# A hybrid decoder layer: the in-projection's first group in a hand-written order, meta tokens transposed together, gates in two passes

## Chip, cores and metric

The kernel runs on one core of one Trainium2 chip. The metric is device time in microseconds (us), the median of several runs. The engines are TensorE (PE, with its weight loads shown apart as PEld), VectorE (DVE), ScalarE (ACT), GpSimd (POOL) and SyncE (SP), which issues most DMAs.

## What is computed

One layer of a hybrid decoder trunk over 16 meta tokens and 256 real tokens of width 2048, in float32. The input is normalised by RMS and multiplied by a gain, then projected by `w_in` into all the inputs of an mLSTM, a stick-breaking attention and a pooling mixer. Their outputs are projected back, and a SwiGLU block follows. The part that matters here:

```python
xn = rmsnorm(h, g_pre)
u = jnp.einsum('bld,de->ble', xn, w_in) * vmask
ml_q, ml_k, ml_v, ml_o, ml_i, ml_f, sb_q, sb_k, sb_v, pool_u = split_cols(u, IN_SIZES)
log_i = jnp.where(vmask, ml_i + ig_b, -jnp.inf)
log_f = jnp.where(vmask, jax.nn.log_sigmoid(ml_f + fg_b), 0.0)
...
return h + token_mixing(h) + channel_mixing(...)   # meta tokens dropped at the end
```

`ml_i` and `ml_f` are the gates, six columns each.

## The kernel before

The contraction over 2048 is cut into 16 k tiles of 128. The activations lie transposed in SBUF, k on the partitions and 272 tokens (16 meta, 256 real) on the free axis. Each float32 operand is split into a high part in the multiplier's format and the rest (`xhi`, `xlo` for the tokens, `hi`, `lo` for the weights), and `mm3` makes a product from three matmuls: hi with hi, hi with lo, lo with hi. `split` makes the weight parts, the high one with a cast on ScalarE, the low one with a subtraction on VectorE. Only four such pairs of buffers exist, and three raw weight buffers.

The in-projection is a list of eleven groups of three or four blocks of 128 output columns, each block with an accumulator of its own in PSUM (`acc0` to `acc3`). The first group holds the blocks sbq0, sbq1 and sbq2 and, in `acc3`, the twelve gate columns. This group also has the work of getting started: a warm-up (eight products of ones with ones, L188, and the gain's transpose, L189), the transposes of x and of the meta tokens (`x_trans`, L209 to L218, three transposes to a k tile), the squares for the RMS (`x_squares`, twelve activations of 512 columns, L207), and `x_norm`, which turns the sums into 1/RMS per token and spreads it over the partitions with matmuls (L232) into `rb`. The gain is multiplied in when the transposed tile leaves PSUM; 1/RMS is multiplied in when a block's accumulator is read (`evac`, for sbq at L491).

The blocks go through chunks of k tiles (0-2, 2-4, 4-8, 8-12, 12-16). After each pair of k tiles the gates get three matmuls for each tile, with 38 weight columns: input gates at columns 0 to 5, forget gates at 32 to 37, and high and low weights in two separate tiles `gw[:, 0]` and `gw[:, 1]`, filled by small copies on ScalarE (L590) and subtractions on VectorE (L591). For the last chunk each block is finished before the next is begun, with `x_norm` behind the first block. `gates` (L281 on) then makes the mLSTM's gate sequences while the second group is running; it reads the gates' accumulator at L287 and, last, at L294. The second group has four blocks, so it needs all four accumulators.

The order on each engine is chosen by the compiler, which goes by its own forecast of times and by the order in the text; DMAs of x, of the meta tokens, of the gain and of the weight chunks are all issued by SP in the order of the text.

Of the kernel before, what the change touches and what calls it, by code (L numbers as in the profile page):

```python
# [37 lines left out]
def tile_hybrid_layer(  # L38
# [33 lines left out]
    def nm(s):  # L72
        uid[0] += 1
        return f"{s}_{uid[0]}"
# [9 lines left out]
    def load(view, nk, w):  # L84
        raw = rawp.tile([P, 2 * MB], F32, tag="raw", name=nm("raw"), bufs=RAWB)
        r = raw[:, : nk * w].rearrange("p (k c) -> p k c", c=w)
        sp.dma_start(out=r, in_=view)
        return r
# [22 lines left out]
    act.preload_act_table_set("natural_log_exp_and_others")  # L111
# [16 lines left out]
    x_v = x.rearrange("o (i p) d -> p (o i) d", p=P)  # L128
    row0 = wk.tile([P, 928], F32, tag="slot1", name="row0", bufs=1)[:16, :P]
# [13 lines left out]
    def load0(a, b):  # L143
        chunks[a] = load(win_view(a, b - a, OG, 396), b - a, 396)
# [16 lines left out]
    pool.dma_start(out=pw, in_=pool_w[0].rearrange("g c d -> c g d"))  # L161

# [16 lines left out]
    gw = big.tile([P, 2, KT, 64], F32R, tag="mixlo", name="gw")  # L179
    pool.memset(gw.bitcast(F32), 0.0)  # L180


    cols = cst.tile([P, 44], F32, name="cols")
    gmc = cst.tile([P, 16], F32, name="gmc")
    pc = mx()
    for _ in range(8):

        pe.matmul(pc[:, :P], lhsT=ones, rhs=ones, start=True, stop=True)  # L188
    pe.transpose(pc[:, :16], row0, ident[:16, :16])  # L189
    vec.tensor_copy(out=gmc, in_=pc[:, :16])  # L190
# [8 lines left out]
    ssx = mp.tile([P, 3, 4], F32, name="ssx")  # L199
    vec.memset(ssx, 0.0)  # L200

    def x_squares():
        for c in range(4):
            cs = slice(c * 512, (c + 1) * 512)
            for i, (src, n) in enumerate(((xin[:, 0, cs], P), (xin[:, 1, cs], P), (mt[:, cs], NMETA))):
                jk = wk.tile([P, 512], BF16, tag="jk", name=nm("jk"), bufs=1)
                act.activation(jk[:n], src, AF.Square, accum_out=ssx[:n, i, c : c + 1])  # L207

    def x_trans(k):  # L209
        pt = mx()  # L210
        ks = slice(k * P, (k + 1) * P)
        pe.transpose(pt[:, 0:NMETA], mt[:, ks], ident[:NMETA, :NMETA])
        pe.transpose(pt[:, NMETA : NMETA + P], xin[:, 0, ks], ident)
        pe.transpose(pt[:, NMETA + P : T], xin[:, 1, ks], ident)
        g = gmc[:, k : k + 1]
        act.activation(xhi[:, k, :], pt[:, :T], AF.Identity, scale=g)
        vec.scalar_tensor_tensor(out=xlo[:, k, :], in0=pt[:, :T], scalar=g, in1=xhi[:, k, :].bitcast(F32),
                                 op0=ALU.mult, op1=ALU.subtract)  # L218

# [61 lines left out]
    def gates(pg):  # L281
# [5 lines left out]
        vec.tensor_tensor(out=f[F], in0=pg[F, :T], in1=rb[F], op=ALU.mult)  # L287
# [6 lines left out]
        vec.tensor_tensor(out=ig[:NH], in0=pg[:NH, :T], in1=rb[:NH], op=ALU.mult)  # L294
# [268 lines left out]
    for gi, blocks in enumerate(groups):  # L563
        nb = len(blocks)
        w = P * nb
        accs = [acc(b) for b in range(nb)]
        pg = acc(3) if gi == 0 else None
        if gi == 0:
            spans = [(0, 2), (2, 4), (4, 8), (8, 12), (12, 16)]
        else:  # L570
            spans = [(4 * c, 4 * c + 4) for c in range(4)]
        for ka, kb in spans:
            if gi == 0:
                for k in range(0 if ka == 0 else kb, min(KT, 2 * kb if kb < 4 else kb + 4)):
                    x_trans(k)
                if ka == 8:
                    x_squares()
                    other_cols()
                r = chunks[ka] if ka in chunks else load(win_view(ka, kb - ka, OG, 396), kb - ka, 396)
            else:  # L580
                r = load_group(ka, kb, blocks)
            subs = []
            for k0 in range(ka, kb, 2):
                rs = r[:, k0 - ka : k0 - ka + 2]
                if gi == 0:
                    gsrc = rs[:, :, 0:12].rearrange("p k (a b) -> p k a b", a=2)
                    dst = [gw[:, j, k0 : k0 + 2, :].rearrange("p k (a b) -> p k a b", a=2)[:, :, :, 0:6]
                           for j in range(2)]
                    for a in range(2):
                        act.copy(out=dst[0][:, :, a], in_=gsrc[:, :, a])  # L590
                        vec.tensor_tensor(out=dst[1][:, :, a], in0=gsrc[:, :, a], in1=dst[0][:, :, a].bitcast(F32),  # L591
                                          op=ALU.subtract)
                    rs = rs[:, :, 12:]
                subs.append((k0, split(rs, 2, w)))
            last = kb == KT
            passes = [subs] if last else [[s] for s in subs]
            for ss in passes:
                for b, (kind, i) in enumerate(blocks):
# [9 lines left out]
                    if last:  # L608
                        if gi == 0 and b == 0:
                            x_norm()  # L610
# [325 lines left out]
```

## Time and profile before

| | us |
|---|---|
| median of 3 runs | 1122.26 (1122.12 to 1122.67) |
| the profiled execution | 1122.67 |
| its span | 1120.5 |
| TensorE busy | 1108.0 (99%) |
| VectorE busy | 700.3 (62%) |
| ScalarE busy | 501.4 (45%) |
| GpSimd busy | 22.8 (2%) |

The span runs from the first to the last instruction of the profiled execution; its time contains some 2.2 us more. Busy times of matmuls overlap, because a matmul is still draining when the next one starts: their pace is read from the spacing of their starts, not from their length. The clock column of the profile starts at full speed where it has no record yet, so in the first microseconds the spacing tells the clock better.

### The profile page before, as it was taken

To read this page: it belongs to the slowest core of one execution; us is meant where nothing else is said; L and a number is where in the kernel's file an instruction comes from. 1 tells how busy PE (TensorE), PEld (TensorE's weight loads), DVE (VectorE), ACT (ScalarE), POOL (GpSimd) and SP (SyncE) were. 2 spreads that over 40 slices of the span, in tenths; PEclk is the share of its full clock that TensorE was granted. 3 is DMA by queue.
4 is the path that set the end of the run, shared out by engine and by line. 5 is a ranking of instruction groups with operands and counts; after the bars stand their busy time and mean duration, and the time that the engine had idled before them with its cause. 6 is when DMAs were issued, how large, how long until landed. Compare 5 with 4: busy or idle time off the path is not lost.

```text
span 1120.5 us, 14565 instructions
## 1 busy us (share of the span) xinstructions
PE 1108.0 (99%) x5863; PEld 956.2 (85%) x5863; DVE 700.3 (62%) x932; ACT 501.4 (45%) x660; POOL 22.8 (2%) x66
## 2 busy tenths in 40 slices
PE   9999999999999999999999999999999999999997
PEld 7999999999988888888888888888888788888885
DVE  4776754768955766576585675774765844454444
ACT  6544444534434664444444444444344534343432
POOL 4000000000000000000000000000000000000000
PEclk9999999999999999999999999999999999999999
DMA  7554643544485655655656655656655555556652
GB/s 244 182 174 145 213 153 114 178 125 131 153 337 188 224 181 178 204 188 189 198 199 194 198 183 193 192 184 206 206 181 195 183 193 189 192 193 199 200 192 75
DMA packets 100548, 208.57 MB, mean 186 GB/s; under 512 B 3963, under 2 KB 31403, under 8 KB 99953
## 3 DMA queue, kind: packets, MB, share of 16 engines
q1 hardware_dynamic: 99168, 201.58, 55.0%
q0 software_dynamic: 896, 2.92, 0.9%
q10 hardware_dynamic: 416, 3.15, 0.7%
q8 instruction: 46, 0.75, 0.3%
q14 instruction: 22, 0.17, 0.0%
HBM read 205.52 MB, written 2.11 MB: 185 GB/s over the span
## 4 chain that ended last, share of the span: by engine, by line
PE 97%; DVE 2%; DMA 0%; ACT 0%; issue 0%; SPq 0%; DVEq 0%; POOLq 0%; ACTq 0%
PE mx L738 8%; PE mx L740 8%; PE mx L739 8%; PE acc L102 7%; PE acc L100 7%; PE acc L101 7%; PE acc L740 6%; PE acc L739 6%; PE acc L738 6%; PE mx L629 5%; PE mx L630 5%; PE mx L628 5%; PE acc L629 5%; PE acc L630 5%; PE acc L628 5%; DVE lo L96 1%
## 5 line engine op out<-in xcount | busy, mean ns | idle before, releaser
L96 DVE TENSOR_TENSOR lo<-raw,hi 128x1024 fp32r<-128x1024 f32 (+1 forms) x384 | 459.1, 1200 | 356.2 <-ACT hi L95 353.2
L95 ACT CAST hi<-raw 128x1024 fp32r<-128x1024 f32 (+1 forms) x384 | 393.8, 1029 | 489.9 <-PE mx L740 124.3
L102 PE MATMUL acc<-xhi,lo 128*128 128x272 f32 (+4 forms) x640 | 192.2, 301 | 0.0
L100 PE MATMUL acc<-xhi,hi 128*128 128x272 f32 (+4 forms) x640 | 187.2, 292 | 0.4 <-DVE im L294 0.4
L101 PE MATMUL acc<-xlo,hi 128*128 128x272 f32 (+4 forms) x640 | 186.7, 292 | 0.0
L738 PE MATMUL mx<-hi,x2hi 128*128 128x512 f32 x384 | 149.6, 390 | 0.0
L740 PE MATMUL mx<-hi,x2lo 128*128 128x512 f32 x384 | 149.6, 390 | 0.0
L739 PE MATMUL mx<-lo,x2hi 128*128 128x512 f32 x384 | 149.4, 389 | 0.0
L738 PE MATMUL acc<-hi,x2hi 128*128 128x512 f32 x320 | 124.5, 389 | 0.0
L739 PE MATMUL acc<-lo,x2hi 128*128 128x512 f32 x320 | 124.5, 389 | 0.0
L740 PE MATMUL acc<-hi,x2lo 128*128 128x512 f32 x320 | 124.5, 389 | 0.0
L100 PEld LDWEIGHTS acc<-xhi,hi 128*128 128x128 f32 x640 | 121.5, 190 | 2.2 <-issue 1.4
L102 PEld LDWEIGHTS acc<-xhi,lo 128*128 128x128 f32 x640 | 121.5, 190 | 1.6 <-issue 1.0
L101 PEld LDWEIGHTS acc<-xlo,hi 128*128 128x128 f32 x640 | 121.4, 190 | 0.3
L738 PEld LDWEIGHTS mx<-hi,x2hi 128*128 128x128 f32 x384 | 72.1, 188 | 15.0 <-ACT x2hi L832 0.3
L740 PEld LDWEIGHTS mx<-hi,x2lo 128*128 128x128 f32 x384 | 72.1, 188 | 14.9
L739 PEld LDWEIGHTS mx<-lo,x2hi 128*128 128x128 f32 x384 | 72.1, 188 | 14.8
L771 DVE STREAM_TRANSPOSE turn<-hg 32x256 f32<-32x256 f32 x176 | 76.7, 436 | 2.8
L739 PEld LDWEIGHTS acc<-lo,x2hi 128*128 128x128 f32 x320 | 60.1, 188 | 12.6
L738 PEld LDWEIGHTS acc<-hi,x2hi 128*128 128x128 f32 x320 | 60.1, 188 | 12.4
L740 PEld LDWEIGHTS acc<-hi,x2lo 128*128 128x128 f32 x320 | 60.1, 188 | 12.4
L629 PE MATMUL acc<-lo,hid 128*128 128x512 f32 x176 | 68.7, 390 | 1.4 <-DVE lo L96 1.4
(225 smaller groups left out, 1252.4 us busy)
## 6 DMA issues: line engine op xcount, KB each, us to landing
raw<-in_w_gate_up_dram SPq DMA_DIRECT2D x88, 1024.0 KB, 5.1
raw<-in_w_down_dram SPq DMA_DIRECT2D x44, 1024.0 KB, 5.2
raw<-in_w_in_dram SPq DMA_DIRECT2D x36, 512.0 KB, 4.8
raw<-in_w_out_dram SPq DMA_DIRECT2D x16, 1024.0 KB, 5.2
raw<-in_w_in_dram SPq DMA_DIRECT2D x12, 1024.0 KB, 5.2
raw<-in_w_in_dram SPq DMA_DIRECT2D x8, 768.0 KB, 4.5
raw<-in_w_in_dram SPq DMA_DIRECT2D x3, 792.0 KB, 6.9
h<-in_x_dram ACTq DMA_DIRECT2D x1, 2048.0 KB, 11.7
```

Source lines behind the costliest of these rows:

```text
L95: act.copy(out=h, in_=r)
L96: vec.tensor_tensor(out=l, in0=r, in1=h.bitcast(F32), op=ALU.subtract)
L100: pe.matmul(o, lhsT=wh, rhs=xh, start=start, stop=False, **kw)
L101: pe.matmul(o, lhsT=wh, rhs=xl, start=False, stop=False, **kw)
L102: pe.matmul(o, lhsT=wl, rhs=xh, start=False, stop=stop, **kw)
L628: pe.matmul(o, lhsT=lh, rhs=h[:, 0, js], start=k == 0, stop=False)
L629: pe.matmul(o, lhsT=lh, rhs=l[:, 0, js], start=False, stop=False)
L630: pe.matmul(o, lhsT=ll, rhs=h[:, 0, js], start=False, stop=k == nk - 1)
L738: pe.matmul(o, lhsT=x2hi[:, k, ts], rhs=h[:, kk, :], start=k == 0, stop=False)
L739: pe.matmul(o, lhsT=x2hi[:, k, ts], rhs=l[:, kk, :], start=False, stop=False)
L740: pe.matmul(o, lhsT=x2lo[:, k, ts], rhs=h[:, kk, :], start=False, stop=k == KT - 1)
L771: vec.transpose(out=dst[32 * j : 32 * j + 32, :, :, a, :], in_=src[32 * a : 32 * a + 32, :, :, j, :])
```

## The change

The first group gets a function of its own, `first_group`, in a region (`manual_schedule`) in which TensorE, ScalarE and VectorE execute in the order of the text. Meta tokens are loaded a second time in the layout (8 k tiles x 16 tokens) x 128 columns and transposed in two transposes instead of sixteen. The gate weights' high and low parts lie side by side in one tile of 102 columns, so that each k tile takes two matmuls instead of three (the product of the two low parts is computed too), and `gates` adds the two halves. The squares are taken in two calls of three activations of 1024 columns, behind the pairs 12 and 14. The warm-up has eleven products, five ahead of the gain's transpose and six behind it. The gain row and the first weight chunk are issued by ScalarE, the meta rows behind the x slices.

```diff
-    sp.dma_start(out=row0, in_=g_mix_pre.rearrange("o (a b) -> (o a) b", b=P))
     load_x(0, 2)
-    sp.dma_start(out=mt, in_=meta)
-    load0(0, 2)
+    act.dma_start(out=row0, in_=g_mix_pre.rearrange("o (a b) -> (o a) b", b=P))
+    load0(0, 2, act)
     load_x(2, 4)
     load0(2, 4)
     load_x(4, 8)
     load0(4, 8)
+    for h in range(2):
+        sp.dma_start(out=mt8[:, h, :], in_=meta[:, h * 1024 : (h + 1) * 1024].rearrange("t (k c) -> k t c", c=P))
     load_x(8, 12)
     load_x(12, 16)
+    sp.dma_start(out=mt, in_=meta)
...
+    gw = big.tile([P, KT, P], F32R, tag="mixlo", name="gw")
+    pool.memset(gw.bitcast(F32), 0.0)
+    act.preload_act_table_set("natural_log_exp_and_others")
...
+    def warm(pc, n):
+        for _ in range(n):
+            pe.matmul(pc[:, P : 2 * P], lhsT=ones, rhs=ones, start=True, stop=True)
+    def gain_column():
+        pc = mx()
+        warm(pc, 5)
+        pe.transpose(pc[:, :16], row0, ident[:16, :16])
+        vec.tensor_copy(out=gmc, in_=pc[:, :16])
+        warm(pc, 6)
...
+    def x_squares(c):
+        cs = slice(c * 1024, (c + 1) * 1024)
+        for i, (src, n) in enumerate(((xin[:, 0, cs], P), (xin[:, 1, cs], P), (mt[:, cs], NMETA))):
+            jk = wk.tile([P, 1024], BF16, tag="jk", name=nm("jk"), bufs=1)
+            act.activation(jk[:n], src, AF.Square, accum_out=ssx[:n, i, c : c + 1])
...
     def x_trans(k):
         pt = mx()
-        pe.transpose(pt[:, 0:NMETA], mt[:, ks], ident[:NMETA, :NMETA])
-        pe.transpose(pt[:, NMETA : NMETA + P], xin[:, 0, ks], ident)
-        pe.transpose(pt[:, NMETA + P : T], xin[:, 1, ks], ident)
+        pe.transpose(pt[:, 0:P], xin[:, 0, ks], ident)
+        pe.transpose(pt[:, P : 2 * P], xin[:, 1, ks], ident)
...
+    def meta_trans():
+        pt = mx()
+        for h in range(2):
+            pe.transpose(pt[:, h * P : (h + 1) * P], mt8[:, h, :], ident)
+        mg = itile(NT).rearrange("p (k t) -> p k t", t=NMETA)
+        vec.tensor_tensor(out=mg, in0=pt[:, : 2 * P].rearrange("p (k t) -> p k t", t=NMETA),
+                          in1=gmc.unsqueeze(2).broadcast_to([P, KT, NMETA]), op=ALU.mult)
+        vec.tensor_copy(out=xhi[:, :, 0:NMETA], in_=mg)
+        vec.tensor_tensor(out=xlo[:, :, 0:NMETA], in0=mg, in1=xhi[:, :, 0:NMETA].bitcast(F32), op=ALU.subtract)
...
-        vec.tensor_tensor(out=f[F], in0=pg[F, :T], in1=rb[F], op=ALU.mult)
+        act.copy(out=e[F], in_=pg[96:102, :T])
+        act.copy(out=ig[:NH], in_=pg[64:70, :T])
+        vec.tensor_tensor(out=f[F], in0=pg[F, :T], in1=e[F], op=ALU.add)
+        vec.tensor_tensor(out=f[F], in0=f[F], in1=rb[F], op=ALU.mult)
...
-        vec.tensor_tensor(out=ig[:NH], in0=pg[:NH, :T], in1=rb[:NH], op=ALU.mult)
+        vec.tensor_tensor(out=ig[:NH], in0=pg[:NH, :T], in1=ig[:NH], op=ALU.add)
+        vec.tensor_tensor(out=ig[:NH], in0=ig[:NH], in1=rb[:NH], op=ALU.mult)
...
+        def w_gates(ka, kb):
+            gsrc = chunks[ka][:, :, 0:12].rearrange("p k (a b) -> p k a b", a=2)
+            dst = gw[:, ka:kb, :].rearrange("p k (s a b) -> p k s a b", s=2, a=2)[:, :, :, :, 0:6]
+            vec.tensor_copy(out=dst[:, :, 0], in_=gsrc)
+            vec.tensor_tensor(out=dst[:, :, 1], in0=gsrc, in1=dst[:, :, 0].bitcast(F32), op=ALU.subtract)
+        def gate_pair(k0):
+            for k in (k0, k0 + 1):
+                pe.matmul(pg[:102, :T], lhsT=gw[:, k, 0:102], rhs=xhi[:, k, :], start=k == 0, stop=False)
+                pe.matmul(pg[:102, :T], lhsT=gw[:, k, 0:102], rhs=xlo[:, k, :], start=False, stop=k == KT - 1)
+        with tc.manual_schedule(engines={mybir.EngineType.PE, mybir.EngineType.Activation, mybir.EngineType.DVE}):
+            gain_column()
+            x_pair(0)
+            w_pair(0)
+            x_pair(2)
+            w_gates(0, 2)
+            w_pair(2)
+            pair(0)
+            x_pair(4)
+            w_gates(2, 4)
+            w_pair(4)
+            pair(2)
+            x_pair(6)
+            w_pair(6)
+            w_gates(4, 8)
+            pair(4)
+            meta_trans()
+            x_pair(8)
+            w_pair(8)
+            pair(6)
+            for k in (0, 2, 4, 6):
+                gate_pair(k)
+            x_pair(10)
+            w_pair(10)
+            w_gates(8, 12)
+            pair(8)
+            gate_pair(8)
+            x_pair(12)
+            w_pair(12)
+            x_squares(0)
+            pair(10)
+            gate_pair(10)
+            x_pair(14)
+            w_pair(14)
+            w_gates(12, 16)
+            x_squares(1)
+            other_cols()
+            for b in range(3):
+                products(accs, blocks, b, [(k, subs[k]) for k in (12, 14)])
+                if b == 0:
+                    x_norm()
+                    gate_pair(12)
+                    gate_pair(14)
+                evac(*blocks[b], accs[b])
+        quick.append([0, gates(pg), None])
```

`x_pair(k)` transposes the tiles k and k+1, `w_pair(k)` splits their weights, `pair(k)` runs their products for the three blocks, 18 matmuls.

## Rows read from the trace of the kernel before

**Rows 1.** Windows: stretch, busy us of each engine (instructions), TensorE clock, DMA share, GB/s.

```profile
42.40:48.00 5.60, 5.22 (x44) 5.04 (x43) 4.03 (x8) 1.71 (x4) 0.00 (x0) 1.00 0.49 148
60.00:1000.00 940.00, 938.38 (x4968) 811.99 (x4967) 610.56 (x802) 423.59 (x535) 6.94 (x11) 1.00 0.57 187
```

**Rows 2.** Timeline of TensorE, 0 to 14 us: start, length, engine, line, operation.

```profile
1.13 3.78 PE L188 MATMUL mx<-ones 128*128 128x128 f32 x16 [1.13 <-DVE ssx L200]
...
6.62 0.28 PE L212 MATMUL mx<-ident,mt 16*128 16x16 f32 x1 [1.50 <-DMA mt<-in_meta_tokens_dram]
...
9.67 0.56 PE L100 MATMUL acc<-xhi,hi 128*128 128x256 f32 x1
...
13.55 0.41 PE L102 MATMUL acc<-xhi,lo 128*128 128x256 f32 x1
```

**Rows 3.** Timeline of TensorE, 14 to 25 us.

```profile
14.46 0.23 PE L212 MATMUL mx<-ident,mt 16*128 16x16 f32 x1
14.62 0.33 PE L213 MATMUL mx<-ident,xin 128*128 128x128 f32 x1
...
14.99 0.23 PE L212 MATMUL mx<-ident,mt 16*128 16x16 f32 x1
...
22.08 0.28 PE L100 MATMUL acc<-xhi,hi 128*128 128x256 f32 x1
...
23.85 0.29 PE L100 MATMUL acc<-xhi,gw 128*38 128x272 f32 x1
...
24.60 0.28 PE L100 MATMUL acc<-xhi,hi 128*128 128x256 f32 x1
```

**Rows 4.** Timeline of TensorE, 37 to 48 us: end of group one, second group.

```profile
37.10 0.93 PE L232 MATMUL mx<-im,ones 128*128 128x128 f32 x6
...
42.39 0.28 PE L100 MATMUL acc<-xhi,hi 128*128 128x260 f32 x1
...
46.56 0.28 PE L102 MATMUL acc<-xhi,lo 128*128 128x256 f32 x1
47.23 0.36 PE L100 MATMUL acc<-xhi,hi 128*128 128x256 f32 x1 [0.38 <-DVE im L294]
```

**Rows 5.** Timeline of ScalarE, 11 to 32 us.

```profile
11.12 0.64 ACT L207 ACTIVATE jk<-xin 128x512 bf16<-128x512 f32 x1
...
11.88 0.63 ACT L207 ACTIVATE jk<-mt 16x512 bf16<-16x512 f32 x1
...
20.33 2.08 ACT L216 ACTIVATE xhi<-mx,gmc 128x272 fp32r<-128x272 f32 x4 [0.19 <-PE mx L214]
...
27.21 0.19 ACT L207 ACTIVATION_READ_ACCUMULATOR jk<-mt 16x1 f32 x1
...
30.17 0.83 ACT L95 CAST hi<-raw 128x768 fp32r<-128x768 f32 x1
30.89 0.30 ACT L590 CAST gw<-raw 128x12 fp32r<-128x12 f32 x2
```

**Rows 6.** Groups by line and form, 0 to 90 us: busy us, mean ns.

```profile
L95 ACT CAST hi<-raw 128x1024 fp32r<-128x1024 f32 x18 | 18.6, 1046 | 22.8 <-PE acc L101 22.8
```

**Rows 7.** DMA issues, 0 to 60 us: KB each, median us to landing.

```profile
xin<-in_x_dram SPq DMA_DIRECT2D x2, 256.0 KB, 4.9
```

**Rows 8.** Waits of SP's queue, 0 to 70 us: us in total, times, longest.

```profile
SPq L87 <- DVE gw L591: 9.8, 2, 9.1
```

**Rows 9.** Timeline of VectorE, 30 to 35 us.

```profile
31.03 0.96 DVE L96 TENSOR_TENSOR lo<-raw,hi 128x768 fp32r<-128x768 f32 x1
...
33.97 0.61 DVE L231 TENSOR_SCALAR im<-ident,r 128x128 f32<-128x128 f32 x3
```

**Rows 10.** Timeline of GpSimd, 26 to 30 us.

```profile
27.88 0.89 POOL L116 TENSOR_TENSOR r<-s,neghalf 128x3 f32<-128x3 f32 x1 [13.64 <-DVE s L115]
```

**Rows 11.** Windows at the end of the kernel, columns as in rows 1.

```profile
1112.00:1114.00 2.00, 0.61 (x3) 0.19 (x1) 0.91 (x3) 0.69 (x2) 0.26 (x1) 1.00 0.74 272
...
1116.50:1117.00 0.50, 0.00 (x0) 0.00 (x0) 0.50 (x2) 0.00 (x0) 0.00 (x0) 0.52 0.99 374
```

More of the change, by code (lines that the diff above doesn't have):

```diff
@@ L196, in other_cols @@
         vec.tensor_copy(out=cols, in_=pc[:, :44])
-    ssx = mp.tile([P, 3, 4], F32, name="ssx")
+    ssx = mp.tile([P, 3, 2], F32, name="ssx")
     vec.memset(ssx, 0.0)
[L202 to L207, printed above, removed]
+    def x_squares(c):
[3 more added lines that the diff above has]
+            act.activation(jk[:n], src, AF.Square, accum_out=ssx[:n, i, c : c + 1])
     def x_trans(k):
@@ L561, in load_group, with products, first_group, x_pair @@
         return r
-    for gi, blocks in enumerate(groups):
+    def products(accs, blocks, b, subs):
+        kind, i = blocks[b]
+        ts = slice(first(kind, i), T)
+        bs = slice(b * P, (b + 1) * P)
+        for k0, (h, l) in subs:
+            for kk in range(2):
+                k = k0 + kk
+                mm3(accs[b][:, : T - ts.start], h[:, kk, bs], l[:, kk, bs], xhi[:, k, ts], xlo[:, k, ts],
+                    k == 0, k == KT - 1)
+            tick()
+    def first_group(blocks):
+        accs, pg = [acc(b) for b in range(3)], acc(3)
+        subs = {}
+        def x_pair(k):
+            x_trans(k)
+            x_trans(k + 1)
+        def w_pair(k):
+            ka = k if k < 4 else k // 4 * 4
+            if k == ka and ka not in chunks:
+                chunks[ka] = load(win_view(ka, 4, OG, 396), 4, 396)
+            subs[k] = split(chunks[ka][:, k - ka : k - ka + 2, 12:], 2, 384)
+        def w_gates(ka, kb):
[3 more added lines that the diff above has]
+            vec.tensor_tensor(out=dst[:, :, 1], in0=gsrc, in1=dst[:, :, 0].bitcast(F32), op=ALU.subtract)
+        def pair(k):
+            for b in range(3):
+                products(accs, blocks, b, [(k, subs[k])])
+        def gate_pair(k0):
[39 more added lines that the diff above has]
+            other_cols()
+            for b in range(3):
+                products(accs, blocks, b, [(k, subs[k]) for k in (12, 14)])
[5 more added lines that the diff above has]
+        quick.append([0, gates(pg), None])
@@ L564, in tile_hybrid_layer @@
+    first_group(groups[0])
+    for blocks in groups[1:]:
         nb = len(blocks)
-        w = P * nb
         accs = [acc(b) for b in range(nb)]
[L567 to L597, printed above, removed]
-                for b, (kind, i) in enumerate(blocks):
-                    ts = slice(first(kind, i), T)
-                    n = T - ts.start
-                    for k0, (h, l) in ss:
-                        for kk in range(2):
-                            k = k0 + kk
-                            bs = slice(b * P, (b + 1) * P)
-                            mm3(accs[b][:, :n], h[:, kk, bs], l[:, kk, bs], xhi[:, k, ts], xlo[:, k, ts],
-                                k == 0, k == KT - 1)
-                        tick()
@@ L608, in tile_hybrid_layer @@
+        for ka in range(0, KT, 4):
+            r = load_group(ka, ka + 4, blocks)
+            subs = [(k0, split(r[:, k0 - ka : k0 - ka + 2], 2, P * nb)) for k0 in (ka, ka + 2)]
+            last = ka + 4 == KT
+            for ss in [subs] if last else [[s] for s in subs]:
+                for b, (kind, i) in enumerate(blocks):
+                    products(accs, blocks, b, ss)
                     if last:
-                        if gi == 0 and b == 0:
-                            x_norm()
```

28 lines of the change are left out of this document (7 added, 21 removed).

## The prediction

> **What bounds the kernel.** I read the windows first. In the long middle TensorE is busy 938.38 of 940.00 us [rows 1], so whatever the first group of the in-projection gains or loses stays in the total: nothing behind it has slack to swallow it. The change touches only that first group, so the question is when TensorE starts the second group. Before, that is at 42.39 us [rows 4]. Then I read TensorE's timeline from the start. It runs eight warm-up products (3.78 us, 0.47 each), pauses until 6.62 for the meta tokens, transposes four k tiles, and begins the products at 9.67 [rows 2]. From there to 42.39 it has no wait. A product of 256 columns comes every 0.23 us from 9.67 to 13.55 (17 steps) and every 0.118 us later (15 steps from 22.08 to 23.85) [rows 2, 3]: about what 256 columns take at 1.2 and at 2.4 GHz, so the clock rose at about 13.8 us. The one wait near the seam stands in the second group: 46.56 + 0.12 to 47.23, about 0.55 us, for the gates' last read of their accumulator [rows 4]; the window there shows 5.22 us busy of 5.60 [rows 1].
>
> ScalarE and VectorE had slack because the compiler slipped the row squares into gaps. The change takes that freedom away: three engines now run the first group in the order written. So I laid each engine's queue out by hand from row durations.
>
> **Work removed from TensorE.** Meta transposes: 16 go, two come. One takes 0.16 us (14.46 to 14.62) of a set of three that takes 0.53 [rows 3]. At that level 16 x 0.16 = 2.6 us go; each new one costs half of the remaining 0.37, so 0.4 comes, net -2.2. Gates: 48 products become 32, at 0.125 us (six from 23.85 to 24.60) [rows 3]: -2.0. Their weights grow from 38 to 102 columns; the nearest row on the other side is the main product, whose 128-column weights step at 0.118 us, so I charge nothing.
>
> **The start.** Five warm-ups (2.35 us from 1.13), a gain transpose (0.28, the level of the meta transposes in [rows 2]), six more (2.82): TensorE is free at about 6.6, where it was at 6.62 before [rows 2]. The first x slice no longer queues behind other loads; issued near 0.8 with a landing time of 4.9 [rows 7], it is there by 5.7, so the longer warm-up eats that head start. The gain row and the first weight chunk move to ScalarE's queue, idle then. The two new meta loads and the other x slices land as before or earlier, and the plain meta rows, now last, are first read near 31 us. The weight chunks of k 8 and 12, whose issue waited 9.8 us for the gate copies [rows 8], come earlier. The gate copies leave ScalarE: ten small operations on VectorE, 0.2 us each by the diagonal of 128 columns in [rows 9], in gaps that my layout leaves there. Clearing the gate tile and loading ScalarE's table move within the first 7 us, ahead of whatever reads them. Where loads share engines a slice may land 1 us later; that is a bound, +0 to +0.5.
>
> From 6.6: x_pair(0) ends its first tile at 7.0; with 0.2 for the drain, two gains on ScalarE at 0.52 (four in 2.08) end at 8.2, the cast of the weights 0.72 (30.17 to 30.89) at 8.9 [rows 5], its low part 0.96 [rows 9] at about 9.9. Two products pass before that, sixteen follow: 9.9 + 16 x 0.118 = 11.8, if the clock is high.
>
> **To the squares.** From 11.8 TensorE has the transposes of five pairs (4, 6, 8, 10, 12) at 4 x 0.185 = 3.7 us, four pairs of products at 18 x 0.118 = 8.5, the meta tokens 0.4, and 20 gate products 2.5: 15.1, so the tiles of k 12 and 13 are transposed at 26.9. None of these waits in my layout: ScalarE idles 1 to 3 us ahead of each pair. (If the meta tokens' strided write into all k rows is held against the reads of neighbouring columns, add up to 1.0 us; I take none, since the column ranges do not meet.)
>
> **The squares, where the gain goes.** In the written order x_squares(0) stands on ScalarE behind the cast of pair 12 and ahead of the gains of pair 14; x_squares(1) stands behind the cast of pair 14; and x_norm's three products stand on TensorE between the last block of sbq0 and everything else. A square with its read of the sum costs 0.76 us at 512 columns (11.12 to 11.88) [rows 5]. At 1024 no row shows it: bounded by 0.76 and twice that. The cast of 1024 takes 1.05 [rows 6] against 0.83 for 768 [rows 5], 0.22 for 256 columns, so I take 0.76 + 0.43 = 1.19, three for 3.6.
>
> ScalarE: the gains of 12 and 13 end 27.8; cast 28.5; squares 32.1; gains of 14 and 15 33.1; cast 33.8; squares 37.4. Then the sums: in the trace the last read ends at 27.21 + 0.19 = 27.40 and the root is done at 27.88 + 0.89 = 28.77 [rows 5, 10], so 1.37: 38.8. The first diagonal 0.2 (three in 0.61) [rows 9]: 39.0. TensorE's x_norm 0.93 [rows 4]: 39.9. Behind it wait 8 gate products (1.0) and 24 products (2.8): the second group starts at 43.7. TensorE itself would have been at the pair 14 products at 31.3 (26.9, then 2.1 of pair 10, 0.5 of gates, 0.7 of transposes, 0.2 of other_cols, 0.7 of pair 12); it waits 2.5 for the cast, 0.8 for the low part and 3.6 for x_norm, some 7 us, more than the change removes.
>
> **The sum.** 43.7 - 42.39 = +1.3. The 0.55 wait in the second group should go: the gates' sums are whole at 40.9, before two blocks of products, so two copies and one more add fit ahead of the 48.0 at which the fourth accumulator is wanted (43.7 + the 4.3 of [rows 4], 42.39 to 46.68). Bound: 0 to -0.55; I take all. In sum +0.75. The profiled execution took 1122.67 us (span 1120.5 and 2.2 around it), 0.4 over the median of 1122.26; the same difference on the median gives 1123.0. Own range of this case: squares of 1.0 to 1.45 move it by -1.1 to +1.6, so 1121.9 to 1124.6. A measurement of this kernel can tell about 0.2%, 2.2 us, from no change, so this case is mostly "same".
>
> **Rivals.**
> *The warm-up does not lift the clock (slower).* My sum needs TensorE at the high level by the first products. In the trace 3.78 us of warm-up and a pause did not lift it; 3.05 us of transposes and 4.1 of products without a break did [rows 2]. The new warm-up is 5.4 us with a transpose in it, running straight into transposes: longer than the one that failed, shorter than the stretch that worked. If it stays low until the products have run about 4 us, 18 products cost 0.11 more each: +2.0, so +2.8 and 1125.0. Against: no pause of 1.5 us stands in it now. Chance 0.27.
>
> *The squares do not hold TensorE (faster).* If ScalarE clears them before TensorE reaches x_norm, the last block goes on when the low part of pair 14 is there: transposes end 30.4, gains 31.6, cast 32.3, low part 33.3, six products 0.7, x_norm 0.9, 3.8 of the rest: 38.7, and with the wait gone -4.2, 1118.0. It decides where the squares end before 32.5. For it: before, they were done by 27.40 [rows 5], fitted between casts, and ScalarE is idle ahead of every pair. Against: the order on the engine is written out, and a half-size effect (one of the two calls out of the way) gives only about 1120. Chance 0.16.
>
> *The clock falls during the wait (slower).* TensorE would stand 3.6 us before x_norm. At the end of the kernel its last product ends at about 1112.6 and the granted clock falls only at about 1116.5 (0.52 over the half microsecond from there) [rows 11]: 3.9 us of idleness, just over what I lay out. If it falls, the 32 products behind x_norm run at 0.23 for 0.12, up to 3.5 us more, about +3 if it rises again before the end: 1126. The Trainium skill (TensorE: Matmul & The Clock Gate, "Why this matters for your kernels") speaks against this change here: it warns that long idle gaps between bursts of matmuls put the clock back to half. By that rule the time would be the 1126 just given; the tail row agrees with the rule in kind, and shows the clock still high for as long as this wait lasts. Chance 0.05.
>
> *The squares are cheaper and nothing else moves*: the lower end of the forecast's own range, 1121.9, within its 0.52.
>
> **Numbers.** Forecast 0.52, clock late 0.27, squares free 0.16, clock falls 0.05. Of the forecast nearly all lies within 0.2%, the clock and wait cases lie above it but for 0.01, the free squares below. Faster 0.17, same 0.52, slower 0.31. The range 1119.8 to 1125.4 leaves out about 0.1 below and 0.1 above.
>
> **What would show it.** Right: TensorE waits in front of the pair 14 products on the cast, then in front of x_norm on the diagonals, 6 to 8 us in all; ScalarE runs six 1024-wide squares between about 28 and 38 us without a gap; second group starts near 43.7; no wait on the gates at the fourth accumulator. The clock step is read from the spacing of the first products, 0.118 or 0.21. Wrong: a start of the second group before 41, or squares done before 31, would mean that the hold was mis-read; products at 0.21 beyond 10 us give the clock case.

## The result, and the profile after

The changed kernel takes 1129.65 us (median of 6 runs, 1127.27 to 1131.32); beside it the kernel before took 1122.55. The ratio is 1.006, with a 95% interval of 1.005 to 1.007: slower by 0.6%, where 1123.0 with a range to 1125.4 was forecast. The profiled execution took 1127.27 us, with a span of 1125.4; it is the quickest of the six. Two more executions, profiled later, took 1131.9 each and are read below.

All of the loss is made in the first group. Counted from the end of the kernel, the same matmul starts 5.2 us later than before at 51 us and still 5.0 us later at 1108 us. So the question is again when the second group starts. The waits of the first 60 us (engine and line, what it waited for: us in total, times, longest):

```profile
PE mx L251 <- DVE im L250: 5.2, 1, 5.2
...
PE acc L102 <- DVE lo L96: 3.0, 3, 1.9
PE acc L100 <- ACT hi L95: 2.9, 2, 2.1
```

The timeline of TensorE shows where these stand; it answers to [rows 2 to 4].

```profile
4.12 2.06 PE L193 MATMUL mx<-ones 128*128 128x128 f32 x12 [0.27 <-DVE gmc L199]
6.01 0.27 PE L222 MATMUL mx<-ident,xin 128*128 128x128 f32 x1
...
9.17 0.39 PE L102 MATMUL acc<-xhi,lo 128*128 128x256 f32 x1 [0.61 <-DVE lo L96]
...
16.46 0.38 PE L102 MATMUL acc<-xhi,lo 128*128 128x256 f32 x1 [1.92 <-DVE lo L96]
...
26.60 0.37 PE L624 MATMUL acc<-xhi,gw 128*102 128x272 f32 x1 [0.65 <-DVE gw L616]
...
34.06 0.38 PE L100 MATMUL acc<-xhi,hi 128*128 128x256 f32 x1 [2.14 <-ACT hi L95]
35.05 0.38 PE L102 MATMUL acc<-xhi,lo 128*128 128x256 f32 x1 [0.49 <-DVE lo L96]
40.96 1.73 PE L251 MATMUL mx<-im,ones 128*128 128x128 f32 x6 [5.17 <-DVE im L250]
...
48.06 0.29 PE L100 MATMUL acc<-xhi,hi 128*128 128x260 f32 x1
```

The second group starts at 48.06, where it was 42.39 before [rows 4] and 43.7 was forecast. The waits at 34, 35 and 41 us were forecast (2.5, 0.8 and 3.6); the ones at 16.46 and 26.60 were not. The cause of the first stands on VectorE (first fence), while GpSimd clears buffers (second fence):

```profile
9.82 0.25 DVE L615 CAST gw<-raw 128x24 fp32r<-128x24 f32 x1
...
12.89 2.44 DVE L615 CAST gw<-raw 128x24 fp32r<-128x24 f32 x1
15.36 0.18 DVE L616 TENSOR_TENSOR gw<-raw,gw 128x24 fp32r<-128x24 f32 x1
15.46 0.95 DVE L96 TENSOR_TENSOR lo<-raw,hi 128x768 fp32r<-128x768 f32 x1
```

```profile
11.20 0.84 POOL L273 MEMSET sbk<- 128x112 f32 x6
...
12.40 1.57 POOL L275 MEMSET mlq<- 128x256 f32 x6
...
14.80 0.95 POOL L277 MEMSET mlv<- 128x128 f32 x6
```

A copy of 24 columns takes 0.25 us before the clears and 2.44 us among them (it ends at 15.33, the last clears at 15.75); the low part of pair 4 queues behind it, and TensorE waits for that. At 26.60 TensorE waits for the gate weights of the tiles 8 to 11, whose copy stands on VectorE behind the low part of pair 10. Then ScalarE's squares, which answer to [rows 5]:

```profile
31.43 1.06 ACT L217 ACTIVATE jk<-mt 16x1024 bf16<-16x1024 f32 x1
...
33.92 1.05 ACT L217 ACTIVATE jk<-xin 128x1024 bf16<-128x1024 f32 x1
...
34.97 1.03 ACT L95 CAST hi<-raw 128x1024 fp32r<-128x1024 f32 x1
35.90 1.05 ACT L217 ACTIVATE jk<-xin 128x1024 bf16<-128x1024 f32 x1
...
36.95 1.03 ACT L95 CAST hi<-raw 128x1024 fp32r<-128x1024 f32 x1
37.89 1.05 ACT L217 ACTIVATE jk<-mt 16x1024 bf16<-16x1024 f32 x1
38.85 0.18 ACT L217 ACTIVATION_READ_ACCUMULATOR jk<-mt 16x1 f32 x1
```

Two casts of 1024 columns, work of the second group, stand between the last three squares. The hand-written order holds among the instructions of the region; the casts come from the text behind it, and the compiler has put them in. The windows (columns as in [rows 1]) show the clock:

```profile
34.00:36.00 2.00, 1.23 (x6) 0.83 (x6) 1.38 (x4) 2.00 (x5) 0.00 (x0) 0.95 0.00 0
36.00:38.00 2.00, 0.00 (x0) 0.00 (x0) 1.23 (x1) 2.00 (x4) 0.00 (x0) 0.50 0.67 170
...
44.00:46.00 2.00, 2.00 (x11) 2.00 (x10) 0.40 (x1) 0.76 (x2) 0.00 (x0) 0.50 0.04 10
46.00:48.00 2.00, 2.00 (x19) 2.00 (x18) 1.56 (x5) 0.57 (x1) 0.00 (x0) 0.99 0.01 4
```

It falls to 1.2 GHz near 35.8 us and comes back near 46.0, so everything behind `x_norm` up to there runs at half pace: 11 matmuls in the window from 44, 19 in the next.

### The profile page after: what moved, and what is told of

It reads as the page before. It is cut to its first block, busy times and chain, and to the rows that moved or that the text cites. A ratio compares the mean times of both kernels' runs of the same rounds, so it can differ in the third digit from the quotient of the medians.

```text
span 1125.4 us, 14497 instructions
## 1 busy us (share of the span) xinstructions
PE 1102.8 (98%) x5839; PEld 953.6 (85%) x5839; DVE 703.6 (63%) x931; ACT 498.5 (44%) x634; POOL 24.3 (2%) x66
## 4 chain that ended last, share of the span: by engine, by line
PE 96%; DVE 2%; ACT 1%; issue 0%; POOL 0%; DVEq 0%; POOLq 0%; ACTq 0%
PE mx L805 8%; PE mx L806 8%; PE mx L807 8%; PE acc L102 7%; PE acc L100 7%; PE acc L101 7%; PE acc L806 6%; PE acc L805 6%; PE acc L807 6%; PE mx L696 5%; PE mx L697 5%; PE mx L695 5%; PE acc L696 5%; PE acc L697 5%; PE acc L695 4%; DVE lo L96 1%
## 5 line engine op out<-in xcount | busy, mean ns | idle before, releaser
L807 PEld LDWEIGHTS mx<-hi,x2lo 128*128 128x128 f32 x384 | 72.1, 188 | 14.9
```

What stands on the lines that cost most here:

```text
L807: pe.matmul(o, lhsT=x2lo[:, k, ts], rhs=h[:, kk, :], start=False, stop=k == KT - 1)
```

## Experiments

The theory: three entries of the written order stand in front of TensorE, and the clock falls while it waits. (A) A gate copy on VectorE stands still while GpSimd clears buffers. (B) The squares are late on ScalarE, with two casts among them. (C) The sum and the root stand, as text, behind all the work of pair 14. The rivals: the compiler's own order would be no better; one entry alone does it; or the clock alone does it.

| version | second group at, us | median (range, runs) | ratio to before (95%) |
|---|---|---|---|
| the change | 48.06 | 1129.65 (1127.27 to 1131.32, 6) | 1.0060 (1.0050 to 1.0070) |
| e1 squares earlier | 47.93 | 1127.09 (1126.46 to 1128.25, 4) | 1.0039 (1.0024 to 1.0054) |
| e2 no written order | 42.58 | 1121.09 (1120.39 to 1122.33, 10) | 0.9987 (0.9978 to 0.9996) |
| e3 `x_norm` last | 47.62 | 1127.11 (1125.52 to 1128.69, 4) | 1.0038 (1.0023 to 1.0053) |
| e4 products in the waits | 48.04 | 1129.14 (1125.15 to 1130.76, 6) | 1.0047 (1.0031 to 1.0064) |
| e5 gate copy on ScalarE | 47.14 | 1128.12 (1127.25 to 1129.87, 4) | 1.0053 (1.0038 to 1.0068) |
| e6 squares and sums earlier | 44.05 | 1123.49 (1120.86 to 1125.46, 10) | 1.0009 (1.0000 to 1.0019) |
| e7 e5 and e6 together, squares apart | 38.76 | 1120.71 (1118.90 to 1122.06, 10) | 0.9981 (0.9972 to 0.9990) |
| e8 clears issued twice | 56.65 | 1135.73 (one run) | |
| e9 e7, meta squares later | 37.27 | 1119.12 (1117.78 to 1120.80, 8) | 0.9969 (0.9959 to 0.9980) |
| e10 e9, short warm-up | 37.85 | 1119.70 (1117.84 to 1121.39, 8) | 0.9975 (0.9965 to 0.9985) |
| e11, e12 the change again | 52.37, 52.79 | 1131.90, 1131.85 (one run each) | |

The start of the second group is that of one profiled execution each; the kernel before took 1122.40 to 1122.55 beside the versions that have an interval, and 1123.26 (one run) beside e11 and e12.

One thing decides how this table is read. In the profiled execution of the change one gate copy took 2.44 us; in those of e1, e3, e4 and e6, as in e11 and e12, it took 4.05 to 4.57. The second groups of these four are therefore to be set against e11 and e12 (52.37 and 52.79), not against 48.06. None of the single moves (e1, e3, e5) nor the products in the waits (e4) brings the second group below 47; e7, which undoes all three entries, has it at 38.76.

**e1: the squares earlier.**

```diff
             w_pair(8)
+            x_squares(0)
...
             w_pair(10)
+            x_squares(1)
...
-            x_squares(0)
...
-            x_squares(1)
```

> Both calls of the squares move forward in the written order: x_squares(0) behind the weights of pair 8, x_squares(1) behind those of pair 10; all else is as changed. Theory H (the late squares hold TensorE, and the waits let the clock fall): no wait over 1 us in front of x_norm, the clock stays at its high level after its first rise, the second group starts near 39.5 us instead of 48.06, and the time is about 1119, 3 us under the kernel before. Rival O (the fixed order costs as a whole, through weights and gate copies that come late): the second group still starts behind 42.4 us and the time stays over 1122.

A miss. The squares are done at 32.8 us, yet TensorE still waits 3.40 us for the diagonals. VectorE's timeline of this version shows why:

```profile
37.43 1.22 DVE L96 TENSOR_TENSOR lo<-raw,hi 128x1024 fp32r<-128x1024 f32 x1
...
38.80 0.15 DVE L243 TENSOR_REDUCE s<-ssx 128x3 f32<-128x6 f32 x1
38.86 1.22 DVE L96 TENSOR_TENSOR lo<-raw,hi 128x1024 fp32r<-128x1024 f32 x1
...
41.17 0.61 DVE L250 TENSOR_SCALAR im<-ident,r 128x128 f32<-128x128 f32 x3 [1.01 <-POOL r L115]
```

TensorE behind it:

```profile
41.60 1.63 PE L251 MATMUL mx<-im,ones 128*128 128x128 f32 x6 [3.40 <-DVE im L250]
```

The reduction waits at its place in VectorE's order, 6 us after its data were there, and two low parts of the second group (1.22 us each) stand around it. So (B) alone does not do it: (C) is behind it. The gate copy took 4.34 us here, and against e11 and e12 the earlier squares do gain: 4.4 to 4.9 us at the second group, part of it because the clock is low for a shorter time (17.8 to 21.2 and 41.7 to 45.1 us).

**e2: the order left to the compiler.** The text stays, the region goes.

```diff
-        with tc.manual_schedule(engines={mybir.EngineType.PE, mybir.EngineType.Activation, mybir.EngineType.DVE}):
+        with ExitStack():
```

> The same text as the changed kernel, but the region that fixes the order on three engines is taken away, so that the compiler orders it as it did before. Theory H: the squares are drawn forward into ScalarE's gaps, no long wait in front of x_norm, second group near 40 to 41 us, time 1119.5 to 1121. Rival O expects the same recovery here but none in the run with the squares moved alone; a third view (the removed work gains nothing) expects 42.4 us and 1122.5.

TensorE has no wait at `x_norm` here. The compiler spread the squares between 10 and 30 us and put the first three gate copies behind the clears, in VectorE's timeline:

```profile
17.23 0.34 DVE L615 CAST gw<-raw 128x24 fp32r<-128x24 f32 x3
```

But it also put the second half of the warm-up at 10.11 us, behind a wait of 5.68, and the clock rose at 18.9 only; the second group comes later than expected (42.58 for 40 to 41). The same operations in another order take 8.6 us less than the change (1121.09 against 1129.65): the order costs the time, not the operations.

**e3: `x_norm` and the last gate products behind all products, the blocks read out after that.**

```diff
             for b in range(3):
                 products(accs, blocks, b, [(k, subs[k]) for k in (12, 14)])
-                if b == 0:
-                    x_norm()
-                    gate_pair(12)
-                    gate_pair(14)
-                evac(*blocks[b], accs[b])
+            gate_pair(12)
+            gate_pair(14)
+            x_norm()
+            for b in range(3):
+                evac(*blocks[b], accs[b])
```

> The squares stay late; x_norm moves behind all products and gate products of the first group, and the three evacuations behind it. Theory H: 32 products (3.8 us) now run under the wait, the wait in front of x_norm shrinks from 5.2 to about 1.5 us, x_norm still ends near 41.5, the second group starts at 43 to 44, time 1123.5 to 1125; whether the clock still falls depends on the 2.1 and 0.5 us waits for pair 14, which stay. Rival O: no more than 1 us gained.

A miss. The wait at `x_norm` shrinks to 0.23 us (at 44.90), but the second group starts at 47.62: the gate copy took 4.34 us, the cast of pair 14 was waited for as before (2.14), the clock was low in three stretches, and a new wait of 1.72 us, for the first block's read-out, stands in front of the second group. Against e11 and e12 that is 4.8 to 5.2 us earlier, so the place of `x_norm` on TensorE matters; but while the entries that feed it are late, the second group stays 5.2 us behind the kernel before.

**e4: products of ones in the waits**, 10 ahead of the products of pair 14 and 22 ahead of `x_norm`, so that TensorE does not stand still.

```diff
-                products(accs, blocks, b, [(k, subs[k]) for k in (12, 14)])
+                products(accs, blocks, b, [(12, subs[12])])
+                if b == 0:
+                    warm(mx(), 10)
+                products(accs, blocks, b, [(14, subs[14])])
                 if b == 0:
+                    warm(mx(), 22)
                     x_norm()
```

> As changed, with warm-up products of ones put on TensorE where it waits: 10 ahead of the products of pair 14, 22 ahead of x_norm. The squares stay late. Theory H with the clock as a part of it: the clock stays at its high level, x_norm starts where it did (41 us) but the 32 products behind it step at 0.12 us, second group near 45.6, time about 1125 instead of 1127 to 1131, and the runs lie closer together. If the fall of the clock has another cause than TensorE's idleness: second group near 48, as changed.

This prices the clock. The two rows are from TensorE's timeline of this version:

```profile
43.21 1.00 PE L251 MATMUL mx<-im,ones 128*128 128x128 f32 x6 [0.26 <-DVE im L250]
...
48.04 0.28 PE L100 MATMUL acc<-xhi,hi 128*128 128x260 f32 x1
```

From `x_norm` to the second group it is 4.83 us, against 7.10 in the change (40.96 to 48.06); the granted clock is 1.00 in every window from 28 to 50 us. The fall costs 2.3 us there. The gate copy took 4.05 us in this execution, and the clock stayed up behind that as well:

```profile
16.13 0.39 PE L102 MATMUL acc<-xhi,lo 128*128 128x256 f32 x1 [3.01 <-DVE lo L96]
```

```profile
17.00:22.00 5.00, 5.00 (x45) 5.00 (x45) 3.70 (x9) 2.24 (x5) 0.00 (x0) 1.00 0.86 311
```

Against e11 and e12 the second group is 4.3 to 4.8 us earlier, in part because their first low stretch (from 17 us) is missing here. A wait of 1.1 us between 380 and 390 us, which stays unexplained, came on top later. The expected 1125 was missed: the medians (1129.14 and 1129.65) are not clear of each other's spread.

**e5: the gate copy on ScalarE.**

```diff
-            vec.tensor_copy(out=dst[:, :, 0], in_=gsrc)
+            act.copy(out=dst[:, :, 0], in_=gsrc)
```

> As changed, with only the copy of the gates' high parts (w_gates) on ScalarE instead of VectorE. New theory P (the copy on VectorE stands still while GpSimd clears buffers: 2.4 to 4.3 us seen, and TensorE's wait of 1.9 to 3.3 us for the weights of pair 4 follows from it, in some runs with a fall of the clock behind it): no VectorE operation over 1.3 us between 9 and 17 us, TensorE's wait for pair 4 under 0.7 us, no low clock between 17 and 21 us; the late squares stay, so the second group still starts at 45 to 47 and the time falls only to 1124 to 1126, with a smaller spread than 1127.3 to 1131.3. Theory H alone (squares): no change, 1127 to 1131.

The wait ahead of pair 4 is gone. The clears still run from 10.4 to 14.9 us, and VectorE's subtractions of the same 24 columns take 0.17 us beside them, the low parts 0.95: only the copy was held. The wait at `x_norm` stays (5.29 us), and the clock falls there as in the change. The second group is 0.9 us earlier than in the first profile of the change and 5.2 to 5.7 us earlier than in e11 and e12. The time, 1128.12, misses the expected 1124 to 1126.

**e6: as e1, and the sums and the root (`x_stats`, taken out of `x_norm`) right behind the gate weights of the tiles 8 to 11.**

```diff
             w_gates(8, 12)
+            x_stats()
```

> The squares moved forward as in the run before (behind pairs 8 and 10), and the sums and the root of x_norm with them, behind the gate copy of k 8 to 11; the three diagonals and products of x_norm stay where they are. The gate copy stays on VectorE. Theory H in its second form (the whole chain squares, sum, root, diagonals must be ahead of TensorE; moving the squares alone left sum and root in VectorE's order behind the weights of pair 14): the wait in front of x_norm falls from 3.4 us to under 0.7, second group near 43.5 to 45 because the gate copy's wait stays, time 1123 to 1125.5. If x_norm's wait stays at 3 us, the form is wrong.

The wait at `x_norm` falls from 3.40 to 1.01 us and the clock stays up there; the second group starts 3.9 us earlier than in e1. The gate copy (4.32 us) and a low clock behind it, 17.6 to 21.1 us, are what is left. That is (C), shown with (B) undone: both executions have the long copy.

**e7: e5 and e6 together, the squares one or two at a time.**

```diff
             w_pair(6)
+            x_squares(0, (0, 1))
...
             w_pair(8)
+            x_squares(1, (0, 1))
...
             w_pair(10)
+            x_squares(0, (2,))
+            x_squares(1, (2,))
             w_gates(8, 12)
+            x_stats()
```

> All three holds taken away at once: gate copy on ScalarE; squares in twos in ScalarE's gaps (behind pairs 6, 8 and 10); sum and root early. H and P together: TensorE has no wait over 1 us behind its first products, clock high throughout from its first rise, second group near 39 us, time 1118.5 to 1120, below the kernel before. If a third hold of a few us is left, it shows as a wait and the time stays over 1121.

The first version in a written order that is below the kernel before (e2 is too): second group at 38.76, 9.3 us earlier than in the first profile of the change, and the clock at 1.00 from 6.1 us on. One entry is still out of place, by TensorE's timeline:

```profile
26.71 0.37 PE L628 MATMUL acc<-xhi,gw 128*102 128x272 f32 x1 [1.89 <-DVE gw L620]
```

The gate copy of the tiles 8 to 11 now stands on ScalarE behind the two meta squares.

**e8: the clears issued twice** (27 by the trace), which only adds work.

```diff
+    for kk in sbk + mlk:
+        pool.memset(kk[:, T:], 0.0)
+    for qq in mlq:
+        pool.memset(qq, 0.0)
+    for vv in sbv + mlv:
+        pool.memset(vv[:, 2, :], 0.0)
```

> As changed, with GpSimd's 21 clearing operations of the attention buffers (4.7 us) issued twice. Theory P: the first or second gate copy on VectorE now ends only when the doubled run of GpSimd ends, near 19.5 us instead of 15.3, so it takes 6 to 9 us, and TensorE's wait for pair 4 grows by some 4 us. Rival (the copy is slow for another reason, its data or its strides): it still takes 2.4 to 4.3 us.

VectorE (first fence) and GpSimd (second) of this version:

```profile
10.73 8.80 DVE L621 CAST gw<-raw 128x24 fp32r<-128x24 f32 x1
19.56 0.18 DVE L622 TENSOR_TENSOR gw<-raw,gw 128x24 fp32r<-128x24 f32 x1
```

```profile
10.42 0.84 POOL L273 MEMSET sbk<- 128x112 f32 x6
...
18.50 0.93 POOL L283 MEMSET mlv<- 128x128 f32 x6
```

The copy begins just after the first clears and ends at 19.53, 0.1 us after the last of them (18.50 + 0.93). With the clears doubled it takes 8.80 instead of the 4.05 to 4.57 us of the executions in which it meets nearly all the clears: they hold it, shown. TensorE waits 6.20 us there.

**e9: e7 with the meta squares behind that gate copy and the sums behind the weights of pair 12.**

```diff
             w_pair(10)
+            w_gates(8, 12)
             x_squares(0, (2,))
             x_squares(1, (2,))
-            w_gates(8, 12)
-            x_stats()
...
             w_pair(12)
+            x_stats()
```

> Gate copy on ScalarE, token squares behind the pairs 6 and 8, meta squares now behind the gate copy of the tiles 8 to 11, sums and root behind the weights of pair 12. In the version before it the gates of tiles 8 to 11 waited 1.89 us, because the two meta squares (2.4 us) stood ahead of their copy on ScalarE, and the second group began at 38.76. Theory H (each stop is only the place of a queue entry): that wait goes, the meta squares end near 26.2 and the gains of pair 12 follow at about 27 as before, so the second group begins 1 to 1.9 us earlier, 36.9 to 37.8, and the time is 1118.8 to 1119.8. Rival B (TensorE was not the late one there; ScalarE is): the wait moves on to the products of pair 10 or 12 behind the same 2.4 us of ScalarE work, the second group begins at 38.4 to 39, time 1120 to 1121.

The wait falls from 1.89 to 0.43 us, and the second group starts 1.5 us earlier, at 37.27: only the place of that entry had been wrong. In this execution it is given back at once, for a new reason. TensorE's timeline and windows of this version:

```profile
44.83 0.22 PE L334 MATMUL mx<-ident,sig 6*128 6x6 f32 x1 [0.97 <-DVE sig L326]
```

```profile
44.00:46.00 2.00, 1.17 (x6) 0.86 (x7) 1.93 (x5) 0.12 (x1) 0.00 (x0) 1.00 0.99 309
...
48.00:50.00 2.00, 2.00 (x11) 2.00 (x11) 0.50 (x1) 1.05 (x1) 0.00 (x0) 0.50 0.69 188
```

In the second group TensorE waits for the gates' next step, and from 47.2 to 50.6 us the clock is low; the lead over the kernel before shrinks from 4.7 us at 51 to 3.15 at 79. In e7 the same wait (0.98) left the clock at 1.00.

**e10: e9 with the warm-up of before.**

```diff
-        warm(pc, 5)
+        warm(pc, 8)
         pe.transpose(pc[:, :16], row0, ident[:16, :16])
         vec.tensor_copy(out=gmc, in_=pc[:, :16])
-        warm(pc, 6)
```

> As the version above, with the warm-up as it was before the change: eight products of ones, all ahead of the gain's transpose. Theory W (the longer warm-up is what lifts the clock before the first products): the first 17 to 40 products come every 0.21 to 0.23 us instead of 0.12, TensorE's clock rises only at some 12 to 14 us, and the second group begins 1 to 3 us later than in the version above. Rival R (the unbroken run of transposes and products lifts it early enough, the first products wait for ScalarE anyway): the spacing is 0.12 by 10 us and the second group begins within 0.5 us of the version above. In time, W gives +1 to +3 us and R less than 0.5 us.

Between the two. TensorE's timeline and a window of this version:

```profile
6.43 0.27 PE L223 MATMUL mx<-ident,xin 128*128 128x128 f32 x1
6.54 0.27 PE L222 MATMUL mx<-ident,xin 128*128 128x128 f32 x1
...
8.87 0.48 PE L102 MATMUL acc<-xhi,lo 128*128 128x256 f32 x1 [0.49 <-DVE lo L96]
```

```profile
10.00:12.00 2.00, 2.00 (x11) 2.00 (x11) 0.75 (x1) 0.00 (x0) 2.00 (x11) 0.50 1.11 329
```

The short warm-up lifts the clock too, here at 5.6 us: the transposes at 6.4 come every 0.11 us. It falls again at 9.0, behind waits of 0.95 and 0.49 us. So the first lo product starts earlier (8.87 against 9.81), but the 15 products behind it come every 0.21 us up to 12.1, and the second group is 0.58 us later. The times (1119.70 and 1119.12) have overlapping intervals. That the longer warm-up prevents this fall is not shown: e8 has the longer one, waits of 0.99 and 0.56 us at the same two places, and the same low stretch, from 10.5 to 14.0 us; its TensorE rows come every 0.21 us there:

```profile
10.07 0.39 PE L102 MATMUL acc<-xhi,lo 128*128 128x256 f32 x1 [0.56 <-DVE lo L96]
...
12.86 0.41 PE L101 MATMUL acc<-xlo,hi 128*128 128x256 f32 x1
13.08 0.41 PE L102 MATMUL acc<-xhi,lo 128*128 128x256 f32 x1
```

**e11 and e12: the changed kernel again, for its profile.**

> The changed kernel once more, unaltered, for its profile: the median of its runs lies 2.4 us over the execution that was profiled, and that part is in no trace so far. Theory V (the first gate copy's place among the clears varies): a run of 1129 us or more has the second gate copy at 4.0 to 4.4 us instead of 2.44 and TensorE's wait behind it at 3.0 to 3.3 instead of 1.92, which gives 1.1 to 1.4 of the 2.4; the rest is a second stretch at the low clock after that wait, some 3.4 us long, 1 to 1.5 us. Rival D (a later part of the kernel): copy and wait as before, second group at 48.1, and the difference arises behind 100 us. A run near 1127.3 says nothing either way.

> As the run above, a second look at the same kernel: theory V gives a copy of 4.0 to 4.4 us and a second group at 49 to 50.5 in a run of 1129 us or more; rival D a second group at 48.1 in any run.

VectorE, TensorE and the windows of e11; e12 is alike (copy 4.32, wait 3.27):

```profile
10.46 4.57 DVE L615 CAST gw<-raw 128x24 fp32r<-128x24 f32 x1
```

```profile
16.17 0.38 PE L102 MATMUL acc<-xhi,lo 128*128 128x256 f32 x1 [3.53 <-DVE lo L96]
...
52.37 0.28 PE L100 MATMUL acc<-xhi,hi 128*128 128x260 f32 x1
```

```profile
18.00:20.00 2.00, 2.00 (x12) 2.00 (x11) 0.08 (x1) 0.13 (x1) 0.00 (x0) 0.50 1.05 379
...
38.00:44.00 6.00, 1.91 (x6) 1.32 (x6) 3.94 (x8) 4.86 (x8) 0.57 (x1) 0.50 0.56 174
```

In these executions it is the first gate copy that is held, not the second: it begins with the first clears and stands for the rest of them. In e11 the wait is 1.6 us longer and TensorE stops in the products of pair 2 instead of pair 4, with a pair more (2.5 us) still to do behind it; the clock is low a first time from about 17 to 20 us, and the second group starts 4.3 us later than in the execution shown first (e12: 4.7). Theory V had the cause right, but with the copy of the tiles 2 and 3 as the one that is held, and a second group at 49 to 50.5. From there on nothing is added (9.5 us behind the kernel before at 51 us, 9.45 at 1108). So the difference between these executions comes from (A) and from the clock, within the first 53 us. Of the six timed runs only the quickest has a trace; that the others, up to 1131.32, had the longer copy is inferred, not shown.

## Why the prediction was wrong

**Right: where the time is decided.** TensorE has no slack behind the first group: in the change, e7, e10, e11 and e12 its distance to the kernel before at 51 us is that at 1108 us within 0.3 us.

**Right: the start.** The clock is up before the first products: transposes come every 0.11 us from 6.0, products every 0.12 from 9.4. The first lo product stands at 9.17, forecast 9.9. The rival "the warm-up does not lift the clock" did not happen. But the longer warm-up was not needed for it: in e10 the short one lifts the clock as well. In the twelve executions in which the transposes follow the warm-up at once the first rise lies between 5.1 and 7.8 us; in the kernel before, with its pause of 1.50 us, it is at 14.0.

**Wrong: "None of these waits in my layout", up to pair 12.** I costed the gate copies at 0.2 us each from a row of VectorE alone and did not look at what GpSimd does meanwhile. One of them took 2.44 us in the first profile and 4.3 to 4.6 in the two others, and TensorE waited 1.92 and 3.3 to 3.5 us behind it. This is the step that failed first. The copy for the tiles 8 to 11 then cost 0.65 us more, by its place in VectorE's queue. Another term was too large: the twenty transposes of the sum, at 0.185 us each (3.7), came every 0.11 (2.2). Together the tiles of k 12 and 13 came at 27.6 instead of 26.9 in the first profile, where these errors partly cancel, and at 31.5 in the two others. What e5 and e8 show is close to a rule of the Trainium skill (SBUF — State Buffer, "SBUF: two separate sides"): VectorE and GpSimd share one pair of ports, and an instruction of either that needs the pair has it alone until it ends. The Trainium skill (VectorE: DVE Perf Modes, "Mode 2×_2P — use both read ports for one tensor") names a copy from SBUF to SBUF among those that use both ports, and a subtraction of two tensors not. The traces agree, with 0.17 us for the subtraction and 2.4 to 8.8 for the copy of the same 24 columns beside the same clears; but the rule speaks of one instruction, and here the copy stood through a row of clears, nearly all 27 in e11 and some 50 in e8. That the ports are the cause, the runs do not show; that the clears hold the copy, they do.

**Right in price, wrong in company: the squares.** One square with its read steps 1.19 us (29.05 to 30.24), as taken. I let them end at 37.4, in a queue with nothing else in it; they end at 39.03. Of the 1.6 us the two casts of the second group take 1.9 (0.93 and 0.94), a start later by 0.55 (29.05 for 28.5) adds to it, and steps within the queue that are shorter than laid out give 0.8 back.

**Right in place, short in length: the hold at `x_norm`.** It is there, 5.17 us for 3.6; root and diagonals took 1.9 us behind the last read for the 1.6 laid out. (The terms laid out for TensorE's arrival at pair 14 add to 31.1, not 31.3; it was ready at 31.76. The forecast goes by ScalarE and does not use that number.) e1 and e6 show that this hold has two causes in a row, the squares and the place of the sums on VectorE, of which I had named only the first: even with the squares done at 32.8 the sums start at 38.8. In the rival "the squares do not hold TensorE" I had taken the squares for the only condition; it gave 1118.0 and a second group at 38.7, which is about where e7 (38.76, 1120.71 us) and e9 (37.27, 1119.12 us) start theirs once both are moved and the copy is too.

**Wrong in its chance: the clock falls during the wait.** I gave it 0.05, because at the end of the kernel 3.9 us of idleness passed before it fell [rows 11]. In the change it fell at 35.8, when TensorE had had waits of 2.14 and 0.49 us with half a microsecond of products between them and the long wait was just beginning. The idle time of one wait is not what decides: in e9 it fell behind a single wait of 0.97 us, in e7 it did not behind the same wait, and in e4 it did not behind one of 3.01. Its price was 2.3 us (e4), where I had 3. The Trainium skill's warning that I weighed there (TensorE: Matmul & The Clock Gate, "Why this matters for your kernels") is of long idle gaps between bursts of matmuls. The traces agree in kind only: the clock did fall, but when the long wait was only beginning, behind the 2.14 and 0.49 us.

**Right: the 0.55 us wait in the second group vanishes.** The fourth block runs on without a gap, and there the distance to the kernel before falls from 5.67 to 5.06 us.

**The sum.** Forecast 43.7 for the second group. `x_norm` came 1.96 late (1.63 from the end of the squares, 0.33 from root and diagonals), and from there it took 7.10 for 4.7, 2.3 of it the clock and 0.1 the rest: 48.06. In the two executions with the long copy it is a further 4.3 and 4.7; in e11 the tiles of k 12 and 13 are 4.6 us late, `x_norm` 5.8 (44.79 for 39.0) and the second group 8.7 (52.37). The work taken away is a gain: the gates take 32 products at 0.125 us while the clock is up, as forecast, and a tile's transposes 0.22 us for 0.53, which over sixteen tiles is more than the 2.2 us laid out; and e9, with every operation of the change and another order of four entries and one engine, is 0.3% faster than the kernel before.

## What to carry to other kernels

An order written by hand takes every entry at its word: for each one, ask not only whether its data are early enough but what stands behind it on its engine, and put sums and roots where their data are ready, not where their result is used. Before a copy moves to VectorE, look at what GpSimd runs in the same microseconds. A tightly packed TensorE can pay twice for a wait, once for the wait and once for the clock (2.3 us in the change, 1.5 in e9). And when executions of one kernel differ, as the change's do here, a profile of a variant is to be set against a profile in which the same thing happened.

## What the runs showed of the hardware

A copy of 128 x 24 float32 on VectorE that takes 0.17 to 0.25 us before or behind the clears took 2.44, 4.05 to 4.57 and, with the clears doubled, 8.80 us while GpSimd cleared buffers. It got through only near the end of the row of clears: 0.4 us before the end in the first profile of the change, 0.1 us behind it in e8 and e11. Subtractions of two tensors ran beside the same clears at their usual 0.17 and 0.95 us.

TensorE's clock fell after waits of 2.14 and 0.49 us in one execution and around a single wait of 0.97 us in another, and it stayed up behind the same wait in a third and behind one of 3.01 us in a fourth (e4). In the change it was back at 46.0, 5.1 us after TensorE had work again; in e9 it was low from 47.2 to 50.6 with TensorE at work throughout. At the start eight products of ones (3.8 us) lifted it when the transposes followed at once (e10), and did not when a pause of 1.50 us came between (the kernel before).
